# Copies for the weight sums moved to the weight queue, their additions queued stage by stage behind POOL's steps

## The chip, the cores and the metric

The kernel runs on one core of a Trainium2 chip. A core has a matrix engine (TensorE, PE in the profile; its weight loads are PEld), a vector engine (DVE), a scalar engine (ACT), a general engine (POOL) and SyncE (SP), which here only issues transfers. Each engine takes its instructions in a fixed order. Transfers (DMAs) are issued from an engine's queue and carried out by 16 shared DMA engines. The metric is the device time of one execution in microseconds (us), as the median of several runs.

## The reference

One decoder layer on 512 tokens of width 2048 in float32, with two groups of heads side by side:

```python
mod = silu(c) @ w_ada + b_ada                       # shift, scale, gate
u = rms_norm(x) * norm_w * (1 + scale) + shift
z, xbc, dt, q, k, v, g = split(u @ w_in)            # w_in is 2048 x 11296
xbc = silu(causal_conv(xbc)); xs, B, C = split(xbc)
y = ssd_scan(xs, softplus(dt + dt_bias), -exp(a_log), B, C) + xs * d_skip
y_ssd = group_rms_norm(y * silu(z)) * ssd_norm_w    # 4 groups of 8 heads
o = retention(rotary(q), rotary(k), v)              # 8 heads, chunks of 128
y_ret = head_norm(o) * ret_norm_w * silu(g)
h = x + gate * (concat(y_ssd, y_ret) @ w_out)       # w_out is 4096 x 2048
out = rms_norm(h) * final_norm_w
```

## The kernel before

**Matrix products.** Every large product is made of three matmuls (`mm3`, L107 to L109): each operand is split into a high part and a low remainder, hi·hi, hi·lo and lo·hi. `load_w` (L93) brings 512 KB of weights with one SP transfer into `raw` (3 buffers), ACT casts it to `hi` (L98), and DVE subtracts to get `lo` (L99; 4 buffers each).

**Stages.** First the modulation vectors, and with them, as far as the activations are ready, the first products (B, C, xs and z of group 0, lines L223 to L277). Then the heads' work. `unit` (L111) is one projection of 512 columns, eight loads of weights and 192 matmuls of 512 columns. For SSD group g: the units xs and z, `ssd_a(g)` (the scan over four chunks: a decay tile loaded by POOL from `acs_d` at L401 and masked at L402, subtracted and multiplied on DVE at L404 and L407, then the matmuls py L419, po L423, pst L432 with `xw` from POOL at L430), and `ssd_b(g)` (gate, square root on POOL at L75 and L76, and `put_mix`, L337, which transposes the result, forms block differences on POOL and stores them to DRAM from POOL's queue). For each pair p of retention heads: the unit qk, `ret_a(p)` (rotary on DVE with an addition on POOL, L468, transposes pk L482, scores), the unit v beside which the gate's weights are loaded, `ret_b(p)` (chunks; a normalisation `mv` on POOL at L75 and L76, state products pkv L537), the unit g, and `ret_c(p)` (gate and `put_mix`). Before the first scan, cumulative decays are computed, transposed and copied to `acsT` (L644), and POOL stores them to `acs_d` in DRAM (L646).

**The output projection** takes `w_out` in 2 x 2 blocks and needs seven block products in place of eight. For that it wants sums of weight blocks, for each of 16 column-by-row pieces j: T1 = B11 + B12, T3 = B12 + B22, T2 = T1 + B22, T4 = T2 + B21. These are made by transfers alone, DRAM to DRAM, 512 KB each: a copy, then transfers that add to their destination, which go through POOL's queue. `block_sums(n)` (L362) issues six stages, one per tick, for pieces n to n − 5: SP copies T1 and T3 (L369); POOL adds to both (L366); POOL copies T1 to T2 (L371); adds (L366); copies T2 to T4 (L373); adds (L366). `unit` calls it at every sixth of its loading steps, over all units counted through.

**Order.** The program order is a priority: a planner lays out each engine's instructions ahead of time from its own estimates of when each is ready, and the engines then run these lists in order. `tc.issue_after(ins)` holds the instructions traced in its block, as far as they are on the engine of `ins`, behind `ins` in that engine's list, without waiting for it to finish. At L122 `ins` is the SP load just issued, so only the SP copies are held by it, and POOL's steps of the sums are placed by the planner.

Of the kernel before, what the change touches and what calls it, by code (L numbers as in the profile page):

```python
# [41 lines left out]
def hybrid_block(ctx, tc, x, c_row, vecs, heads, w_mod, w_gate, b_gate, w_in, w_dt, w_out, fnw,  # L42
                 rope, dmask, xi, zeta, gdec, out):
    nc = tc.nc
    act, dve, pool, pe, sp = nc.scalar, nc.vector, nc.gpsimd, nc.tensor, nc.sync
# [45 lines left out]
    last_load = [None]  # L91
# [19 lines left out]
    def unit(name, w_stationary, tag="mm", side=None):  # L111
        width = 512
        nb = width // P if w_stationary else NC
        banks = [bank(tag, f"acc{b}") for b in range(nb)]
        held = []
        for kc in range(NK // 2):
            held.append((kc, *load_w(w_in[name][kc], width)))
            if side is not None:
                side(kc)
            n = next(steps)  # L120
            if n % 6 == 0:
                with tc.issue_after(last_load[0].ins):  # L122
                    block_sums(n // 6)
            if kc == NK // 2 - 2:
                continue
            for b in range(nb):
                sl = slice(b * P, (b + 1) * P)
                for k, hi, lo in [(2 * c + kt, h[:, kt, :], l[:, kt, :])
                                  for c, h, l in held for kt in range(2)]:
                    if w_stationary:  # L130
                        mm3(banks[b], (hi[:, sl], lo[:, sl]), (uh[k], ul[k]),
                            k == 0, k == NK - 1)
                    else:
                        mm3(banks[b][:, :width], (uh[k][:, sl], ul[k][:, sl]), (hi, lo),
                            k == 0, k == NK - 1)
            held = []
        return banks
# [183 lines left out]
    QJ = 8  # L321
# [4 lines left out]
    B11, B12, B22, B21 = (lambda j, i=i: w_out[4 * j + i] for i in range(4))  # L326
# [32 lines left out]
        pool.dma_start(mixd["SA"][j][:, 1, :], a12)  # L359
        pool.dma_start(mixd["A22"][j // 2][:, j % 2, :], a22)  # L360

    def block_sums(n):  # L362


        def add(dst, src):
            pool.dma_start(dst, src, accum_op=ALU.add, max_dma_last_dim=4096)  # L366

        stages = (
            lambda j: (sp.dma_start(T1(j), B11(j)), sp.dma_start(T3(j), B12(j))),  # L369
            lambda j: (add(T1(j), B12(j)), add(T3(j), B22(j))),  # L370
            lambda j: pool.dma_start(T2(j), T1(j)),  # L371
            lambda j: add(T2(j), B22(j)),
            lambda j: pool.dma_start(T4(j), T2(j)),  # L373
            lambda j: add(T4(j), B21(j)))
        for i, stage in enumerate(stages):
            if 0 <= n - i < 2 * QJ:
                stage(n - i)

    steps = iter(range(10000))


    def ssd_a(g):
        bt, ct, xs = bct[("B", g)], bct[("C", g)], xst[g]
        hs = slice(g * HPG, (g + 1) * HPG)
        pb = bank("aux", "pb")
        for c in range(NC - 1):
            pe.transpose(pb[:, c * P:(c + 1) * P], bt[:, c * P:(c + 1) * P], ident)
        bn = t2k("bn", 2, "bn")
        act.copy(bn[:, 0:3 * P], pb[:, 0:3 * P])
        pcb = bank("aux", "pcb")  # L390
        for c in range(NC):
            sl = slice(c * P, (c + 1) * P)
            pe.matmul(pcb[:, sl], lhsT=bt[:, sl], rhs=ct[:, sl], start=True, stop=True)
        cbt = t2k("cbt", 2, "cbt")
        act.copy(cbt, pcb)
        prev = None
        ys = []
        for c in range(NC):
            sl = slice(c * P, (c + 1) * P)
            dec = t2k("dec", 2, "dec", (P, HPG, P))  # L400
            pool.dma_start(dec, acs_d[c, hs, :].partition_broadcast(P))  # L401
            pool.affine_select(dec, dec, [[0, HPG], [1, P]], ALU.is_ge, -1e30, base=0,  # L402
                               channel_multiplier=-1)
            dve.tensor_tensor(dec, dec, acs[:, c, hs].unsqueeze(2).to_broadcast([P, HPG, P]),  # L404
                              ALU.subtract)
            act.activation(dec, dec, AF.Exp)
            dve.tensor_tensor(dec, dec, cbt[:, sl].unsqueeze(1).to_broadcast([P, HPG, P]), ALU.mult)  # L407
            px = bank("aux", "px")
            for i in range(4):
                pe.transpose(px[:, i * P:(i + 1) * P], xs[i][:, sl], ident)  # L410
            xd = t2k("xd", 2, "xd")
            dve.tensor_tensor(v8(xd), v8(px), bcast_h(dtt[:, c, hs]), ALU.mult)
            xc = t2k("xc", 2, "xc")
            act.copy(xc, px)
            pool.tensor_tensor(v8(xc), v8(xc), bcast_h(dsk[:, hs]), ALU.mult)
            py = bank("aux", "py")
            for h in range(HPG):
                hd = slice(h * 64, (h + 1) * 64)
                pe.matmul(py[:, hd], lhsT=dec[:, h, :], rhs=xd[:, hd], start=True, stop=True)  # L419
            y = t2k("y", 4, "y")  # L420
            if c:
                po = bank("aux", "po")
                pe.matmul(po, lhsT=ct[:, sl], rhs=prev, start=True, stop=True)  # L423
                dve.tensor_tensor(v8(y), v8(po), bcast_h(ea[:, c, hs]), ALU.mult)
                pool.tensor_tensor(xc, xc, y, ALU.add)
            dve.tensor_tensor(y, py, xc, ALU.add)
            ys.append(y)
            if c < NC - 1:
                xw = t2k("xw", 2, "xw")
                pool.tensor_tensor(v8(xw), v8(xd), bcast_h(dte[:, c, hs]), ALU.mult)  # L430
                pst = bank("aux", "pst")
                pe.matmul(pst, lhsT=bn[:, sl], rhs=xw, start=True, stop=True)  # L432
                new = t2k("prev", 2, "new")
                if c == 0:
                    act.copy(new, pst)
                else:
                    pool.tensor_tensor(v8(new), v8(prev), bcast_h(cdec[:, c, hs]), ALU.mult)
                    dve.tensor_tensor(new, pst, new, ALU.add)
                prev = new
        return ys  # L440

    def silu2(pb, name, zs=None):
        th = t2k("th", 2, "th")
        act.activation(th, pb, AF.Tanh, scale=0.5)
        if zs is None:
            zs = t2k("zs", 4, name)
        dve.scalar_tensor_tensor(zs, th, 1.0, pb, ALU.add, ALU.mult)  # L447
        return zs

    def ssd_b(g, ys, zss):  # L450
        sq = small.tile([P, NC], F32, name="sq")
        for c in range(NC):
            y = ys[c]
            dve.tensor_tensor(y, y, zss[c], ALU.mult)
            act.activation(zss[c], y, AF.Square, accum_out=sq[:, c:c + 1])
            rsqrt_into(sq[:, c:c + 1], sq[:, c:c + 1], 1.0 / 2048.0, EPS)
            dve.tensor_scalar(y, y, sq[:, c:c + 1], None, ALU.mult)
        for i in range(4):
            put_mix(4 * g + i, [y[:, i * P:(i + 1) * P] for y in ys], hv(V_SNW, 4 * g + i))
# [106 lines left out]
    def gate_part(n, q):  # L566
        raw = wp.tile([P, 2, 512], F32, tag="raw", bufs=3, name="graw")
        sp.dma_start(raw.rearrange("p k f -> p (k f)"), w_gate[8 * n + q])
        if n % 2 == 0 and q == 0:
            gates["t"] = t2k("dec", 2, "gacc", (P, HPG, P)).rearrange("p (a h) t -> p a (h t)", a=2)  # L570
        if q == 0:
            gates[n] = gates["t"][:, n % 2, :]
        gacc = gates[n]
        for kk in range(2):
            k = 2 * q + kk
            if k == 0:
                dve.tensor_scalar(gacc, raw[:, kk, :], cs[:, k:k + 1], None, ALU.mult)
            else:
                dve.scalar_tensor_tensor(gacc, raw[:, kk, :], cs[:, k:k + 1], gacc,  # L579
                                         ALU.mult, ALU.add)  # L580
# [11 lines left out]
    zs0 = []  # L592
# [59 lines left out]
    for j in range(2):  # L652
        bct[("B", j)] = conv_silu(None, 16 + j, "bc", 5, f"B{j}", aw[j])
        bct[("C", j)] = conv_silu(None, 20 + j, "bc", 5, f"C{j}", aw[2 + j])
    ssd_b(0, ssd_a(0), zs0)
    for g in range(1, GROUPS):
        if g == 2:
            take_bc(unit("BC2", True), 2)
        take_xs(unit(f"xs{g}", True), g)
        ys = ssd_a(g)  # L660
        zb = unit(f"z{g}", False)
        ssd_b(g, ys, [silu2(zb[c], f"zs{c}") for c in range(NC)])
    for p in range(RH // 2):
        qk = unit(f"qk{p}", True)
        a = ret_a(p, qk)
        vb = unit(f"v{p}", False, side=lambda kc: gate_part(p, kc))
        gate_done(p)
        ys = ret_b(p, a, vb)
        gb = unit(f"g{p}", False)
        ret_c(p, ys, gb)  # L670


    gate = []
# [228 lines left out]
```

## Time and profile before

| | |
|---|---|
| runs | 1552.52, 1552.04, 1546.27 us; median 1552.04 |
| profiled execution | 1547.64 us, its span 1545.9 us |
| busy | TensorE 1450.1 us (94%), DVE 890.8 (58%), ACT 539.5 (35%), POOL 395.0 (26%) |
| mean granted TensorE clock | 0.979 of full speed |
| transfers | 324.09 MB; SP's queue 245.52 MB, POOL's 75.37 MB |
| DMA engines' busy share | SP's queue 46.3%, POOL's 20.1% |

A line of the tables of waits names the waiting engine and instruction, what released it, the total in us, how often, and the longest. A line of the timeline gives start, duration, engine, source line, operation, output<-inputs, and in brackets the idle time ahead of it with what ended it. A stretch's line gives its bounds and length, the busy time of PE, PEld, DVE, ACT and POOL, the granted clock, the DMA engines' busy share and GB/s. Of a transfer's issue the profile gives the size and the median time to landing.

### The profile page before, as it was taken

The page shows a single profiled execution, that of the slowest core. Times are in us where ns is not written, and L with a number is a line of the kernel's source. Part 1 is how long each engine was busy: PE and PEld are TensorE (multiplying, and loading weights), DVE is VectorE, ACT ScalarE, POOL GpSimd, SP SyncE. Part 2 cuts the span into 40 slices and gives each one's busy share as a digit, 9 for nine tenths or more (in the row PEclk, how much of TensorE's full clock was granted, in tenths as well). Part 3 has the DMA queues.
Part 4 walks back from the last instruction along what each step waited for, and adds up shares of the span by engine and source line. Part 5 has one row for each costly group of instructions (what it writes and reads, how often), then busy time and mean ns, then how long its engine had stood idle before and what let it go on. Part 6 is the DMA issues. An engine that isn't in the chain of part 4 may idle for free.

```text
span 1545.9 us, 17183 instructions
## 1 busy us (share of the span) xinstructions
PE 1450.1 (94%) x6481; PEld 1177.1 (76%) x6481; DVE 890.8 (58%) x1064; ACT 539.5 (35%) x732; POOL 395.0 (26%) x472
## 2 busy tenths in 40 slices
PE   6989996898999999988998999999999999999997
PEld 4767884686877877766887888788878878888885
DVE  6899764855655455363326433743354456557585
ACT  6433442432433332211121222122222345546454
POOL 4540114565425515432143003200310020000001
PEclk9999997999999999999999999999999999999998
DMA  9887786386787775688687525523553588778755
GB/s 363 321 303 282 226 239 176 116 245 183 216 232 202 228 214 147 211 245 249 182 228 224 159 82 170 172 80 96 171 170 119 166 307 286 248 242 264 248 177 196
DMA packets 86263, 324.09 MB, mean 210 GB/s; under 512 B 11298, under 2 KB 11474, under 8 KB 81058
## 3 DMA queue, kind: packets, MB, share of 16 engines
q1 hardware_dynamic: 66834, 245.52, 46.3%
q0 software_dynamic: 18192, 75.37, 20.1%
q10 hardware_dynamic: 1152, 2.10, 0.4%
q8 instruction: 51, 0.84, 0.2%
q14 instruction: 34, 0.27, 0.0%
HBM read 304.00 MB, written 86.05 MB: 252 GB/s over the span
## 4 chain that ended last, share of the span: by engine, by line
PE 52%; DMA 22%; DVE 13%; issue 6%; POOL 5%; ACT 2%; SPq 0%; DVEq 0%; POOLq 0%; ACTq 0%
PE acc L108 9%; PE acc L107 9%; PE acc L109 9%; DMA T<-w_out_d 9%; DMA graw<-w_gate_d 5%; DVE ada L193 4%; DMA T<-T 4%; PE U L108 4%; PE U L109 4%; PE U L107 3%; PE W L107 3%; PE W L108 3%; PE W L109 3%; DVE lo L99 2%; DVE ul L210 1%
## 5 line engine op out<-in xcount | busy, mean ns | idle before, releaser
L98 ACT CAST hi<-raw 128x1024 fp32r<-128x1024 f32 (+1 forms) x184 | 186.1, 1016 | 448.6 <-PE acc L109 198.7
L99 DVE TENSOR_TENSOR lo<-raw,hi 128x1024 fp32r<-128x1024 f32 (+1 forms) x166 | 211.3, 1277 | 223.8 <-ACT hi L98 223.2
L107 PE MATMUL acc<-hi,uh 128*128 128x512 f32 x704 | 277.5, 396 | 11.0 <-DVE rt L467 10.7
L108 PE MATMUL acc<-lo,uh 128*128 128x512 f32 x704 | 280.2, 398 | 0.0
L109 PE MATMUL acc<-hi,ul 128*128 128x512 f32 x704 | 279.0, 396 | 0.0
L109 PE MATMUL acc<-uh,lo 128*128 128x512 f32 x512 | 201.0, 393 | 0.0
L107 PE MATMUL acc<-uh,hi 128*128 128x512 f32 x512 | 200.7, 394 | 0.3 <-DVE zs L447 0.3
L108 PE MATMUL acc<-ul,hi 128*128 128x512 f32 x512 | 200.7, 392 | 0.0
L735 DVE TENSOR_TENSOR lo<-raw,hi 128x1024 fp32r<-128x1024 f32 x112 | 137.6, 1234 | 81.2 <-ACT hi L734 81.2
L107 PEld LDWEIGHTS acc<-hi,uh 128*128 128x128 f32 x704 | 133.3, 189 | 41.0 <-DVE rt L467 13.0
L734 ACT CAST hi<-raw 128x1024 fp32r<-128x1024 f32 x112 | 117.6, 1054 | 126.7 <-PE W L109 53.8
L109 PEld LDWEIGHTS acc<-hi,ul 128*128 128x128 f32 x704 | 133.6, 190 | 27.9 <-issue 0.2
L108 PEld LDWEIGHTS acc<-lo,uh 128*128 128x128 f32 x704 | 133.6, 190 | 27.9 <-issue 0.5
L107 PEld LDWEIGHTS acc<-uh,hi 128*128 128x128 f32 x512 | 96.6, 189 | 20.9 <-DVE zs L447 1.5
L109 PEld LDWEIGHTS acc<-uh,lo 128*128 128x128 f32 x512 | 96.7, 189 | 19.6
L108 PEld LDWEIGHTS acc<-ul,hi 128*128 128x128 f32 x512 | 96.5, 188 | 19.5
L366 POOL DMA_DIRECT2D T<-w_out_d x64 | 55.3, 886 | 212.4 <-DMA T<-T 107.3
L108 PE MATMUL U<-lo,mh 128*128 128x512 f32 x256 | 99.8, 390 | 0.8 <-DVE lo L735 0.8
L109 PE MATMUL U<-hi,ml 128*128 128x512 f32 x256 | 99.6, 390 | 0.0
L107 PE MATMUL U<-hi,mh 128*128 128x512 f32 x256 | 95.2, 390 | 0.0
L579 DVE SCALAR_TENSOR_TENSOR gacc<-graw,cs,gacc 128x512 f32<-128x512 f32 x60 | 49.4, 823 | 79.2 <-DMA graw<-w_gate_d 78.0
L193 DVE SCALAR_TENSOR_TENSOR ada<-ada,csb 128x2048 f32<-128x2048 f32 x32 | 91.0, 2845 | 0.2 <-DMA ada<-w_mod_d 0.2
(245 smaller groups left out, 2199.8 us busy)
## 6 DMA issues: line engine op xcount, KB each, us to landing
ada<-w_mod_d SPq DMA_DIRECT2D x32, 1024.0 KB, 6.1
T<-w_out_d POOLq DMA_DIRECT2D x64, 512.0 KB, 6.8
raw<-T SPq DMA_DIRECT2D x64, 512.0 KB, 4.3
raw<-w_out_d SPq DMA_DIRECT2D x48, 512.0 KB, 4.4
raw<-w_in_z SPq DMA_DIRECT2D x32, 512.0 KB, 5.1
T<-w_out_d SPq DMA_DIRECT2D x32, 512.0 KB, 6.4
T<-T POOLq DMA_DIRECT2D x32, 512.0 KB, 5.0
raw<-w_in_qk SPq DMA_DIRECT2D x32, 512.0 KB, 3.7
```

Of the source, the lines that this page charges most:

```text
L98: act.copy(hi, raw)
L99: eng.tensor_tensor(lo, raw, hi.bitcast(F32), ALU.subtract)
L107: pe.matmul(dst, lhsT=ah, rhs=bh, start=first, stop=False, skip_group_check=more)
L108: pe.matmul(dst, lhsT=ah, rhs=bl, start=False, stop=False, skip_group_check=more)
L109: pe.matmul(dst, lhsT=al, rhs=bh, start=False, stop=last, skip_group_check=more)
L193: dve.scalar_tensor_tensor(ada, ada, 0.5, csb, ALU.mult, ALU.mult, accum_out=dst)
L210: dve.tensor_tensor(l_k, xT[k], h_k.bitcast(F32), ALU.subtract)
L366: pool.dma_start(dst, src, accum_op=ALU.add, max_dma_last_dim=4096)
L579: dve.scalar_tensor_tensor(gacc, raw[:, kk, :], cs[:, k:k + 1], gacc, ALU.mult, ALU.add)
L734: act.copy(dst[0], src)
L735: dve.tensor_tensor(dst[1], src, dst[0].bitcast(F32), ALU.subtract)
```

## The change

The call of `block_sums` leaves `unit`. It is made instead after each part of the heads' work: `ssd_a`, `ssd_b`, `ret_a`, `ret_b`, `ret_c`, 20 calls (ticks) in all. The six stages become four. At its first tick a piece j has all four T filled by SP copies straight from the weights: T1 from B11, T3 from B12, T2 from B22, T4 from B21. At the second POOL adds B12 to T1 and B22 to T3, at the third T1 to T2, at the fourth T2 to T4. A helper `behind(eng)` finds the instruction last traced on an engine: the copies are held behind SP's last one, the additions behind POOL's last one. Tick 14 issues pieces 14 and 15 together.

```diff
@@ unit
-            n = next(steps)
-            if n % 6 == 0:
-                with tc.issue_after(last_load[0].ins):
-                    block_sums(n // 6)
@@ block_sums
-    def block_sums(n):
+    ticks = iter(range(1000))
+    def behind(eng):
+        ins = next(i for i in reversed(nc.cur_bb.bb.instructions) if i.engine == eng.engine)
+        return tc.issue_after(ins)
+    def block_sums():
         def add(dst, src):
             pool.dma_start(dst, src, accum_op=ALU.add, max_dma_last_dim=4096)
-        stages = (
-            lambda j: (sp.dma_start(T1(j), B11(j)), sp.dma_start(T3(j), B12(j))),
-            lambda j: (add(T1(j), B12(j)), add(T3(j), B22(j))),
-            lambda j: pool.dma_start(T2(j), T1(j)),
-            lambda j: add(T2(j), B22(j)),
-            lambda j: pool.dma_start(T4(j), T2(j)),
-            lambda j: add(T4(j), B21(j)))
-        for i, stage in enumerate(stages):
-            if 0 <= n - i < 2 * QJ:
-                stage(n - i)
-    steps = iter(range(10000))
+        n = next(ticks)
+        for i in range(4):
+            for j in {14: (14, 15)}.get(n - i, (n - i,)):
+                if not 0 <= j < 2 * QJ or n - i > 14:
+                    continue
+                if i == 0:
+                    with behind(sp):
+                        for dst, src in ((T1, B11), (T3, B12), (T2, B22), (T4, B21)):
+                            sp.dma_start(dst(j), src(j))
+                else:
+                    with behind(pool):
+                        if i == 1:
+                            add(T1(j), B12(j))
+                            add(T3(j), B22(j))
+                        elif i == 2:
+                            add(T2(j), T1(j))
+                        else:
+                            add(T4(j), T2(j))
@@ the heads' work
-    ssd_b(0, ssd_a(0), zs0)
+    ys = ssd_a(0)
+    block_sums()
+    ssd_b(0, ys, zs0)
+    block_sums()
     for g in range(1, GROUPS):
...
         ys = ssd_a(g)
+        block_sums()
...
         ssd_b(g, ys, [silu2(zb[c], f"zs{c}") for c in range(NC)])
+        block_sums()
     for p in range(RH // 2):
         qk = unit(f"qk{p}", True)
         a = ret_a(p, qk)
+        block_sums()
...
         ys = ret_b(p, a, vb)
+        block_sums()
         gb = unit(f"g{p}", False)
         ret_c(p, ys, gb)
+        block_sums()
```

## The prediction

> **What bounds the kernel now.** I read the page first: its busy shares, and the chain that ended last by line.
>
> ```profile
> span 1545.9 us, 17183 instructions
> PE 1450.1 (94%) x6481; PEld 1177.1 (76%) x6481; DVE 890.8 (58%) x1064; ACT 539.5 (35%) x732; POOL 395.0 (26%) x472
> ...
> PE acc L108 9%; PE acc L107 9%; PE acc L109 9%; DMA T<-w_out_d 9%; DMA graw<-w_gate_d 5%; DVE ada L193 4%; DMA T<-T 4%; PE U L108 4%; PE U L109 4%; PE U L107 3%; PE W L107 3%; PE W L108 3%; PE W L109 3%; DVE lo L99 2%; DVE ul L210 1%
> ```
>
> TensorE is the bound: 94% busy, and no change to the sums removes a matmul. What can be won is idle TensorE time, 95.8 us in all, and time at a lower clock. The chain, though, runs 13% of the span through transfers into T (9% from the weights, 4% from T to T), which only the output projection reads. So I asked next who waits for T, when T is written and read (the instructions of that tile, with the start of the first and the last), and where TensorE's idle time lies, in stretches cut at the stages.
>
> ```profile
> POOL T L366 <- DMA T<-T: 107.3, 26, 7.0
> POOL T L366 <- DMA T<-w_out_d: 104.5, 20, 19.3
> ...
> POOL T L373 <- DMA T<-w_out_d: 69.8, 16, 6.3
> POOL T L371 <- DMA T<-w_out_d: 55.4, 15, 9.5
> ```
>
> ```profile
> L366 POOL DMA_DIRECT2D T<-w_out_d x64: 797/864/1422, 177.7 to 847.1; - x64
> L739 SPq DMA_DIRECT2D raw<-T x64: 319/320/430, 1214.8 to 1509.0; - x64
> ```
>
> ```profile
> 160.00:236.00 76.00, 76.00 (x349) 62.85 (x349) 51.96 (x80) 31.57 (x47) 12.50 (x20) 1.00 0.79 230
> 236.00:300.00 64.00, 43.37 (x200) 33.52 (x199) 45.11 (x48) 21.71 (x31) 34.05 (x38) 0.84 0.51 132
> 300.00:420.00 120.00, 112.54 (x526) 90.46 (x525) 70.94 (x70) 42.83 (x63) 68.36 (x81) 0.97 0.74 216
> 420.00:555.00 135.00, 131.96 (x622) 107.39 (x622) 73.74 (x86) 51.16 (x72) 52.48 (x67) 0.99 0.79 224
> 555.00:650.00 95.00, 89.98 (x420) 71.57 (x419) 40.44 (x46) 27.39 (x38) 43.13 (x54) 0.98 0.66 184
> 650.00:860.00 210.00, 192.94 (x850) 157.69 (x849) 99.67 (x124) 41.41 (x47) 55.42 (x72) 0.97 0.77 223
> 860.00:1240.00 380.00, 375.22 (x1695) 309.95 (x1694) 175.04 (x246) 98.11 (x119) 59.24 (x79) 1.00 0.43 138
> ```
>
> POOL stands 337.0 us in its queue before T steps (107.3 + 104.5 + 69.8 + 55.4). Columns after the stretch: its length, busy PE, PEld, DVE, ACT, POOL, granted clock, DMA share, GB/s. TensorE idles 20.6, 7.5, 3.0, 5.0 and 17.1 us in the five stretches from 236 to 860, and its clock is below 1 in each. From 860 on, after POOL's last T step at 847, the retention heads do the same kind of work with 4.8 us idle in 380 us at a clock of 1.00. That is a control inside this trace: without T steps in POOL's queue the heads hardly stop TensorE. Last, what TensorE waited for from 160 to 1250:
>
> ```profile
> PE py L419 <- DVE dec L407: 15.2, 1, 15.2
> PE pst L432 <- POOL xw L430: 10.7, 6, 4.4
> PE acc L107 <- DVE rt L467: 10.7, 7, 2.6
> PE pT L342 <- DVE y L457: 7.2, 5, 3.8
> PE pkv L537 <- DVE yr L529: 6.3, 1, 6.3
> PE pk L482 <- POOL r L468: 4.8, 4, 2.0
> ```
>
> The largest is one wait, and the timeline shows its cause.
>
> ```profile
> 219.00 0.27 ACT L644 COPY acsT<-pat 128x128 f32<-128x128 f32 x1
> ...
> 235.27 0.80 POOL L366 DMA_DIRECT2D T<-w_out_d  x1 [6.47 <-DMA T<-T]
> 235.80 0.86 POOL L646 DMA_DIRECT2D acs_d<-acsT  x1
> 241.55 1.08 POOL L401 DMA_DIRECT2D dec<-acs_d  x2 [4.89 <-DMA acs_d<-acsT]
> ...
> 251.74 3.67 PE L419 MATMUL py<-xd,dec 128*128 128x64 f32 x16 [15.18 <-DVE dec L407]
> ...
> 283.53 2.00 PE L419 MATMUL py<-xd,dec 128*128 128x64 f32 x16 [0.89 <-DVE xd L412]
> ```
>
> acsT is ready at 219.3, but its store (L646) stands in POOL's queue behind T steps, each waiting some 6 us for the one before, until 235.8: 16.5 us late. The decay tiles and the first py follow from it.
>
> **The change part by part.** *The six-step chain becomes four, and 32 T-to-T copies leave POOL.* T2 and T4 start as copies of B22 and B21 on SP; POOL then adds T1 and T2. Still 64 copies and 64 additions of 512 KB: the transfers' bytes do not change.
>
> ```profile
> L366 POOL DMA_DIRECT2D T<-w_out_d x64 | 55.3, 886 | 212.4 <-DMA T<-T 107.3 <-DMA T<-w_out_d 104.5 <-issue 0.5
> ...
> L373 POOL DMA_DIRECT2D T<-T x16 | 8.6, 540 | 69.8 <-DMA T<-w_out_d 69.8
> L371 POOL DMA_DIRECT2D T<-T x16 | 8.5, 529 | 55.4 <-DMA T<-w_out_d 55.4
> ...
> T<-w_out_d POOLq DMA_DIRECT2D x64, 512.0 KB, 6.8
> ...
> T<-w_out_d SPq DMA_DIRECT2D x32, 512.0 KB, 6.4
> ```
>
> POOL loses 17.1 us of issue (8.6 + 8.5), worth nothing by itself on an engine 26% busy, and the 125.2 us of waits before these copies.
>
> *The additions go behind POOL's last step of each part, one stage a tick.* From tick 1 on a projection unit lies between two ticks, 192 matmuls, some 42 us at the 349 in 76.0 us of 160:236; an addition lands in a median 6.8 us, so every input has long landed. I cost POOL's waits for T at nothing; the cover is that spacing, and if two ticks fell together each stage would wait up to 6.8 us again. At tick 0 POOL gets no addition, so L646 issues when acsT is there, at about 219.3. Then the store, loads, mask and decay (251.7 − 235.8 = 15.9 us in the trace) give py at 235.2, just before TensorE runs out of other work at 236.6 (251.74 − 15.18). So **15.2 us** of idle go, and the slow restart: 16 py take 3.67 us there and 2.00 later, with the steps behind them about **2.5**.
>
> *The other SSD stalls.* pst waits for xw on POOL 10.7 us; two of the six had no T wait in front of them, so 10.7 − 0.45 − 1.35 = **8.9** go.
>
> ```profile
> 276.30 1.12 PE L432 MATMUL pst<-xw,bn 128*128 128x512 f32 x2 [0.45 <-POOL xw L430]
> ...
> 595.24 1.13 PE L432 MATMUL pst<-xw,bn 128*128 128x512 f32 x2 [1.35 <-POOL xw L430]
> ```
>
> pT waits 7.2 for a normalisation whose square root is on POOL; I credit half, **3.6**. Clock, (1 − clock) × stretch: 3.6 in 300:420, 1.4 in 420:555, 1.9 in 555:650, and, as an estimate of the same size, 1.6 in 236:300 after pT's longest stall of 3.8: **8.5**.
>
> *The first four heads.* 650:860 against its control: idle 17.1 − 4.8 = **12.3** and clock 0.03 × 210 = **6.3**. pkv's 6.3 and the excess in rt and pk are inside this.
>
> Sum of what can go: 15.2 + 2.5 + 8.9 + 3.6 + 8.5 + 12.3 + 6.3 = 57.3 us. The Trainium skill (TensorE: Matmul & The Clock Gate, Part 1) has the clock halve after an idle window of about 3.4 us; by that only the four longest stalls would cost clock, and the sum would be some 5 us smaller (an estimate); but 420:555, with no such gap among its waits, also shows 0.99.
>
> *What it adds: bursts on SP.* Ticks 0 and 1 both stand behind the last load of the first stage, so eight copies, 4.2 MB, go ahead of the xs1 weights; tick 14 also sends eight, the others four.
>
> ```profile
> 168.03 0.33 SPq L95 DMA_DIRECT2D raw<-w_in_xs0b  x1
> 168.63 0.33 SPq L95 DMA_DIRECT2D raw<-w_in_xs  x1
> 169.01 2.84 SPq L369 DMA_DIRECT2D T<-w_out_d  x2
> ...
> 190.19 0.50 PE L107 MATMUL acc<-uh,hi 128*128 128x512 f32 x1
> ...
> 193.03 1.13 SPq L369 DMA_DIRECT2D T<-w_out_d  x2
> ```
>
> The first xs1 load was issued at 168.6 and first used at 190.2: 21.6 us of cover, less about 2.3 for the cast and the subtraction. At the 230 GB/s of 160:236 the eight take 18.2 us. 168.6 + 18.2 + the load's own 2.3 at that rate, + 2.3, makes 191.4: 1 us late, and ACT, held in its cast, may pass it on to acsT. Bounds: 0 (the POOL transfers that shared those 230 GB/s are gone) and 5; I take 2. Later bursts of four take 9.1 us with a like cover: 0.
>
> *What waits behind the additions.* Four take about 3.5 us (4 × 0.886; tick 15 has six, behind ret_b). After ssd_a their successors are ssd_b's square roots, three times (groups 1 to 3), and TensorE waits for those in pT: 0 to 10.5, taken at 5, since the z unit's matmuls cover part. After ret_a, ret_b, ssd_b and ret_c a whole projection unit covers them: 0. The T steps now reach into 860 to about 1130, where the DMA share was 0.43. The first read of T is at 1215, so nothing in the output projection becomes late.
>
> *What passes to the next releaser.* A stalled head often has DVE or ACT a little behind POOL; of the 42.1 us other than the first stall I take off a fifth, 8.
>
> 57.3 − 2 − 5 − 8 = 42 us. The profiled execution took 1547.6 us (span 1545.9 and 1.7 around it): 1547.6 − 42 = 1505.6. The median of the runs shown is 4.4 us above that execution, so I add 2: **1508 us**.
>
> **The rivals.** *Only the first stall goes* (1540): POOL's waits elsewhere hid DVE and ACT chains, and the additions cost their whole 10.5. For it: four of the six rows of TensorE's waits name DVE, not POOL. Against it: the control. 1547.6 − 17.7 + 10.5 is 1540.4.
>
> *The transfers bind and nothing moves* (1548): same bytes, share 0.74 to 0.79 in three of the stretches; waits for T become waits for weights. Against it: TensorE's list of waits names no load. The skill (DMA: Bandwidth & Descriptors, Issuing engines are not separate DMA queues) speaks for it: handing transfers to another issuer saves only issue time.
>
> *The bursts starve TensorE* (1645, slower): the place is the first weights behind a burst. If each copy is served alone in its 6.4 us, four take 25.6 and eight 51.2. Against 19.3 us of cover (21.6 − 2.3) that is 6.3 us in each of the 12 bursts of four and 31.9 in each of the two of eight: 139; 1505.6 + 139 = 1645. It decides from 4.9 us a copy (12 × 0.3 + 2 × 19.9 = 43, the whole gain). Against it: 230 GB/s makes 2.3 us a copy, and pairs issued together, two in 1.13 us, have that 6.4 as their median.
>
> **How the numbers follow.** Forecast 0.62, first stall only 0.18, nothing moves 0.09, starved 0.11. Within 0.5% of 1552 is about what a measurement can tell from no change; so faster 0.80, same 0.09, slower 0.11. The likeliest case's own range is 1490 (all 57.3) to 1530. For 8 in 10 it reaches over the first-stall case to 1546, and down to 1486 for a planner that places the freed work better.
>
> **What would show it.** Right: no T-to-T transfer on POOL, POOL's waits for T below 40 us, L646 within 2 us of acsT, no PE wait above 5 us from 236 to 860, clock 1.00 at 650:860. Wrong step by step: a PE wait for hi or lo near 190 (burst); pT waits above 7.2 us (additions ahead of ssd_b); py still over 10 us late (the order of the planner, not T). The whole is wrong if POOL's waits vanish and TensorE's idle time does not.

## The result and the profile after

| | before | after |
|---|---|---|
| median, us (runs) | 1551.0 (4, 1546.27 to 1552.52) | 1492.65 (4, 1489.38 to 1496.37) |
| profiled execution, us | 1547.64 | 1496.37 |
| its span, us | 1545.9 | 1494.7 |
| mean granted TensorE clock | 0.979 | 0.987 |

The ratio of after to before is 0.963, 95% interval 0.960 to 0.966: 58.4 us between the medians, 51.3 between the two profiled executions. The forecast of 1508 us had the direction and the mechanism, and its range (1486 to 1546) holds the result; the gain was larger than the 42 us worked out.

The page of after, its busy shares and the shares of the chain that ended last by line:

```profile
span 1494.7 us, 17196 instructions
PE 1438.2 (96%) x6481; PEld 1174.4 (79%) x6481; DVE 895.1 (60%) x1064; ACT 540.2 (36%) x732; POOL 377.2 (25%) x440
...
PE acc L108 13%; PE acc L107 13%; PE acc L109 13%; DMA graw<-w_gate_d 5%; DVE ada L189 4%; PE U L108 3%; PE U L109 3%; PE U L107 3%; PE W L107 2%; PE W L108 2%; PE W L109 2%; DVE gacc L588 1%; DVE lo L99 1%; PE py L428 1%; DVE ul L206 1%
```

Transfers into T, which held 13% of the chain, are no longer among the lines listed. TensorE's idle time fell from 95.8 to 56.5 us (1494.7 − 1438.2). Where it went shows in the stretches, before and then after. The bounds are cut at the same stages; columns as in the prediction.

```profile
236.00:860.00 624.00, 570.79 (x2613) 460.62 (x2612) 329.91 (x371) 184.50 (x250) 253.44 (x312) 0.96 0.72 206
860.00:1240.00 380.00, 375.22 (x1695) 309.95 (x1694) 175.04 (x246) 98.11 (x119) 59.24 (x79) 1.00 0.43 138
1240.00:1545.90 305.90, 291.97 (x1279) 240.67 (x1277) 195.83 (x216) 155.22 (x204) 12.33 (x20) 0.98 0.74 245
```

```profile
160.00:236.00 76.00, 76.00 (x349) 63.02 (x348) 55.92 (x85) 34.09 (x50) 10.49 (x14) 1.00 0.59 208
236.00:300.00 64.00, 59.19 (x295) 47.62 (x295) 48.13 (x53) 27.30 (x41) 36.97 (x41) 0.97 0.42 146
300.00:404.00 104.00, 103.83 (x494) 85.08 (x493) 65.71 (x67) 40.76 (x57) 51.07 (x59) 1.00 0.67 194
404.00:530.00 126.00, 126.00 (x607) 103.66 (x606) 76.53 (x85) 49.50 (x70) 45.40 (x56) 1.00 0.63 193
530.00:620.00 90.00, 88.64 (x427) 72.40 (x426) 47.15 (x53) 26.66 (x36) 41.99 (x52) 1.00 0.67 192
620.00:810.00 190.00, 183.48 (x821) 149.60 (x819) 89.11 (x113) 38.65 (x45) 45.01 (x56) 0.99 0.74 217
...
236.00:810.00 574.00, 561.13 (x2637) 458.37 (x2636) 326.62 (x368) 182.87 (x248) 220.43 (x261) 0.99 0.66 196
810.00:1188.00 378.00, 372.62 (x1671) 308.71 (x1672) 178.91 (x246) 97.85 (x119) 77.16 (x103) 0.99 0.63 187
1188.00:1494.70 306.70, 292.39 (x1278) 240.45 (x1276) 195.65 (x216) 155.25 (x204) 11.59 (x19) 0.98 0.75 245
```

From 236 to the end of the heads both kernels run the same 4308 matmuls (2613 + 1695, 2637 + 1671), in 1004 us before and 952 after: 52.0 us. The output projection took 0.8 us longer, and everything before 236 is unchanged. Of the 52.0, idle time gave 39.7 (53.2 + 4.8 before, 12.9 + 5.4 after), and the remaining 12.3 is shorter busy time of the same matmuls; how much of it is clock is worked out below.

The list of TensorE's waits after, from 150 to 1195, and then the one row of a T step in the list of POOL's waits:

```profile
PE acc L107 <- DVE rt L476: 6.4, 6, 2.3
PE pT L338 <- DVE y L433: 4.6, 1, 4.6
PE pk L491 <- POOL r L477: 2.8, 1, 2.8
PE acc L107 <- ACT hi L98: 2.4, 2, 1.2
...
PE acc L108 <- DVE lo L99: 1.5, 2, 0.8
```

```profile
POOL T L369 <- DMA mixAS<-m: 1.6, 1, 1.6
```

The rest of the list are waits of 1.9 us or less in total; py's 15.2, pst's 10.7 and pkv's 6.3 us have no successor in it. The rows for `hi` and `lo`, 3.9 us of waits for weights, are new: they come at 656 and at 809, in the first two v units, behind bursts of four copies. POOL's 337.0 us of waits for T are gone: the 1.6 us ahead of a T step are not for a transfer that makes T. (The list also puts POOL's 48.4 us ahead of `cosb`, until 165.7, down to a transfer into T. The same wait was 47.4 us long before, put down to DVE there, so it is not a new one.) The timeline of after at the first scan, to be held against the one in the prediction:

```profile
221.65 0.27 ACT L653 COPY acsT<-pat 128x128 f32<-128x128 f32 x1 [2.23 <-PE pat L651]
222.21 0.55 POOL L655 DMA_DIRECT2D acs_d<-acsT  x1 [52.65 <-ACT acsT L653]
...
238.78 1.90 PE L428 MATMUL py<-xd,dec 128*128 128x64 f32 x16
```

POOL now waits for acsT (52.7 us, harmless) instead of acsT waiting for POOL. The store goes 0.3 us after acsT, and py runs without an idle gap and at full speed: 1.90 us for the sixteen, 3.67 before.

### The profile page after: what moved, and what is told of

It is laid out like the page before. It is cut to its first block, busy times and chain, and to the rows that moved or that the text cites. A ratio compares the mean times of both kernels' runs of the same rounds, so it can differ in the third digit from the quotient of the medians.

```text
span 1494.7 us, 17196 instructions
## 1 busy us (share of the span) xinstructions
PE 1438.2 (96%) x6481; PEld 1174.4 (79%) x6481; DVE 895.1 (60%) x1064; ACT 540.2 (36%) x732; POOL 377.2 (25%) x440
## 4 chain that ended last, share of the span: by engine, by line
PE 64%; DVE 13%; DMA 10%; issue 8%; POOL 3%; ACT 1%; SPq 1%; DVEq 0%; POOLq 0%; ACTq 0%
PE acc L108 13%; PE acc L107 13%; PE acc L109 13%; DMA graw<-w_gate_d 5%; DVE ada L189 4%; PE U L108 3%; PE U L109 3%; PE U L107 3%; PE W L107 2%; PE W L108 2%; PE W L109 2%; DVE gacc L588 1%; DVE lo L99 1%; PE py L428 1%; DVE ul L206 1%
## 5 line engine op out<-in xcount | busy, mean ns | idle before, releaser
L109 PEld LDWEIGHTS acc<-uh,lo 128*128 128x128 f32 x512 | 96.2, 188 | 19.3
L588 DVE SCALAR_TENSOR_TENSOR gacc<-graw,cs,gacc 128x512 f32<-128x512 f32 x60 | 54.2, 904 | 73.2 <-DMA graw<-w_gate_d 72.1
L108 PE MATMUL W<-lo,mh 128*128 128x512 f32 x192 | 75.6, 394 | 0.1
```

Of the source, the lines that this page charges most:

```text
L108: pe.matmul(dst, lhsT=ah, rhs=bl, start=False, stop=False, skip_group_check=more)
L109: pe.matmul(dst, lhsT=al, rhs=bh, start=False, stop=last, skip_group_check=more)
```

## The experiments

Two edits came together: the chain of six stages became four, and the steps moved from the counter in `unit` to ticks between the parts, with POOL's additions held behind POOL's last step. The first four runs take these apart and take the sums away; the next four look at where the waits stand and at the bursts of copies. All ratios are to the kernel before (median 1549.31 beside the first four, 1550.84 beside the others), with their 95% intervals.

**Six stages at the new place.**

```diff
-        for i in range(4):
+        for i in range(6):
...
-                        for dst, src in ((T1, B11), (T3, B12), (T2, B22), (T4, B21)):
+                        for dst, src in ((T1, B11), (T3, B12)):
...
                         elif i == 2:
-                            add(T2(j), T1(j))
-                        else:
-                            add(T4(j), T2(j))
+                            pool.dma_start(T2(j), T1(j))
+                        elif i == 3:
+                            add(T2(j), B22(j))
+                        elif i == 4:
+                            pool.dma_start(T4(j), T2(j))
+                        else:
+                            add(T4(j), B21(j))
```

> The new places with the old chain: ticks after each part and additions (with both T-to-T copies) held behind POOL's last step, but six stages, so 32 copies stay on POOL. Theory A (what counts is that nothing in POOL's queue waits for a transfer just issued; every stage's input is one part old): POOL's waits for T stay below 40 us, TensorE's idle time as in the changed kernel; 1493 to 1500 us, the 17 us of issue for the copies lying off the path. Rival B (the shorter chain and the copies taken off POOL are the gain): well above, 1520 to 1540 us.

Measured 1492.47 us, ratio 0.963 (0.959 to 0.967): the changed kernel's time, and rival B is out. With the long chain, and its 32 copies still on POOL, the one wait ahead of a T step is this, and no transfer ends it:

```profile
POOL T L369 <- issue: 0.9, 2, 0.5
```

So the shorter chain, and the 32 copies that went from POOL to SP, are worth nothing once the steps stand at the new place, behind POOL's last step. That is also what the Trainium skill says of such a move (DMA: Bandwidth & Descriptors, Issuing engines are not separate DMA queues: it saves only issue time), and here the trace agrees. What it was used for in the prediction's second rival doesn't follow, though: the gain never lay in the issuer.

**Four stages at the old place.**

```diff
-            lambda j: (sp.dma_start(T1(j), B11(j)), sp.dma_start(T3(j), B12(j))),
+            lambda j: [sp.dma_start(d(j), s(j)) for d, s in ((T1, B11), (T3, B12), (T2, B22), (T4, B21))],
             lambda j: (add(T1(j), B12(j)), add(T3(j), B22(j))),
-            lambda j: pool.dma_start(T2(j), T1(j)),
-            lambda j: add(T2(j), B22(j)),
-            lambda j: pool.dma_start(T4(j), T2(j)),
-            lambda j: add(T4(j), B21(j)))
+            lambda j: add(T2(j), T1(j)),
+            lambda j: add(T4(j), T2(j)))
```

> The four-stage chain alone, called from the units' loading steps as before, additions placed by the planner. Theory A: two of six waits per piece are gone, POOL still stands some 200 us for T and still holds up the store of acsT; 1515 to 1535 us. Rival B: 1490 to 1500 us.

Measured 1518.69 us, ratio 0.976 (0.970 to 0.983): 31 us less, about half of the change. The size is uncertain, 27 to 46 us by the interval, and its four runs lie between 1504.55 and 1528.23. POOL's waits, the first scan, and TensorE's stretch over it:

```profile
POOL T L366 <- DMA T<-w_out_d: 206.8, 39, 21.0
...
POOL T L366 <- DMA T<-T: 78.5, 14, 8.2
```

```profile
219.17 0.60 POOL L644 DMA_DIRECT2D acs_d<-acsT  x1 [0.71 <-ACT acsT L642]
...
236.01 1.90 PE L417 MATMUL py<-xd,dec 128*128 128x64 f32 x16
```

```profile
236.00:300.00 64.00, 58.41 (x286) 46.88 (x285) 43.67 (x51) 26.43 (x39) 35.75 (x37) 0.95 0.56 159
```

POOL still waits 285.3 us for T, more than the 200 expected. But it does not hold up the store of acsT, as was expected: the shorter chain was over just as acsT came, and the first sixteen py run at 236.0, without a gap and at full speed, where they came at 251.7 before. TensorE idles 5.6 us from 236 to 300 in place of 20.6. With the steps where the planner puts them, then, a shorter chain counts; some 15 of its 31 us of gain come from this one meeting, which is a matter of timing.

**The ticks without the hold on POOL.** The additions are no longer held behind POOL's last step; the planner places them. SP's copies stay as they were.

```diff
                 else:
-                    with behind(pool):
+                    with nullcontext():
```

> The changed kernel with the additions not held behind POOL's last step (ticks, four stages and SP's holds kept). Theory A: the planner may put an addition as soon as its own estimate of the transfer is over, earlier than the chip lands it; POOL's waits for T come back in part, 50 to 200 us, and 1500 to 1530 us. Rival C (the tick after a part is enough, the hold adds nothing): 1490 to 1497 us.

Measured 1502.47 us, ratio 0.969 (0.965 to 0.974), 10 us above the changed kernel.

```profile
POOL T L369 <- DMA T<-w_out_d: 160.7, 32, 24.4
POOL T L369 <- DMA T<-T: 56.6, 10, 7.6
```

The planner brings the additions forward, and POOL waits 217.3 us, a little more than the 50 to 200 expected. Little of that reaches TensorE. The time is inside theory A's range, and the four runs (1498.41 to 1503.9) lie above all four of the changed kernel, so rival C is out.

**No sums at all.** The transfers into T are gone, and the output projection reads B11, B22, B12 and B21 where it read T1 to T4: the same loads and matmuls on other numbers.

```diff
-            n = next(steps)
-            if n % 6 == 0:
-                with tc.issue_after(last_load[0].ins):
-                    block_sums(n // 6)
...
-    for sweep, (f, wu, ww) in enumerate((("AS", B11, T1), ("SR", T2, B22), ("SA", T3, B21))):
+    for sweep, (f, wu, ww) in enumerate((("AS", B11, B11), ("SR", B22, B22), ("SA", B12, B21))):
...
-        held.append((j, m, weight(T4(j))))
+        held.append((j, m, weight(B21(j))))
```

> The kernel before with no block sums at all: the 128 transfers into T are left out, and the projection reads the weight blocks B11, B22, B12 and B21 where it read T1 to T4, so the output is not the reference's. It gives the price of the sums. Theory A: the changed kernel hides nearly all of it, so this is 1482 to 1492 us, at most 10 us under the changed kernel. Rival D (the transfers' bytes bind, and the changed kernel still pays for 64 copies and 64 additions): below 1475 us.

Measured 1490.67 us, ratio 0.961 (0.958 to 0.965). The sums cost the kernel before some 59 us and the changed one about 2, which is inside the spread of its runs. The rival in which the bytes bind is out: 128 transfers of 512 KB are hidden, once no urgent work stands in line behind them. There is hardly anything left to win in the sums.

**The old steps, four ticks later.** This moves the first steps from 177.7 to 326.6, past the first scan, and changes nothing else.

```diff
-                    block_sums(n // 6)
+                    block_sums(n // 6 - 4)
```

> The kernel before with its sums begun four ticks (24 loading steps) later, so that none stands ahead of the store of acsT; six stages, old places, planner's positions. It isolates the first stall. Theory A (two terms, the first stall with its restart and the waits inside the later parts): the first wait of 15 us goes, the others move to later groups and heads; 1525 to 1537 us. Rival E (the first stall is nearly the whole): 1495 to 1510 us. Rival F (a stall avoided there returns elsewhere): 1545 us or more.

Measured 1538.04 us, ratio 0.993 (0.990 to 0.997), 1 us above theory A's range; rivals E and F are out. Rows of the waits of POOL and TensorE, and the two stretches:

```profile
POOL acs_d L646 <- ACT acsT L644: 50.5, 1, 50.5
...
PE pkv L537 <- DVE yr L529: 15.5, 2, 10.9
```

```profile
236.00:860.00 624.00, 589.83 (x2725) 478.37 (x2723) 327.83 (x378) 189.13 (x256) 240.58 (x296) 0.98 0.71 205
860.00:1190.00 330.00, 311.45 (x1383) 256.84 (x1384) 146.79 (x211) 73.80 (x87) 66.58 (x92) 0.97 0.55 163
```

The store of acsT is in time, so the first stall is gone, which the prediction priced at 17.7 us. The kernel gains only 10 (1 − 0.9934 of 1551) to 13 (the medians). The last of POOL's T steps now comes at 985, in heads that were free of them before, and the largest wait of TensorE is now pkv's, 15.5 us in place of 6.3. There, from 860 to 1190, TensorE idles 18.6 us, against 4.8 in the whole 860:1240 of before. The same heads with T steps in POOL's list stall, without them they don't; this is the prediction's control, now made by an edit.

**Sixteen copies at once.** SP's copies of four pieces go out together at ticks 0, 4, 8 and 12; the additions stay.

```diff
-            for j in {14: (14, 15)}.get(n - i, (n - i,)):
-                if not 0 <= j < 2 * QJ or n - i > 14:
+            js = {14: (14, 15)}.get(n - i, (n - i,) if n - i < 14 else ())
+            if i == 0:
+                js = range(n, n + 4) if n % 4 == 0 else ()
+            for j in js:
+                if not 0 <= j < 2 * QJ:
                     continue
```

> The changed kernel with the copies of four pieces, 16 transfers or 8.4 MB, sent together at ticks 0, 4, 8 and 12; the additions as in the changed kernel. It prices the cover ahead of the weights. By the prediction's figures 16 copies at 230 GB/s take 36.5 us against 19.3 us of cover: some 17 us lost at each of four bursts, 1545 to 1565 us. If copies are served at their packets' pace when nothing else runs (4 KB in 0.159 us on each of 16 engines, 1.3 us a copy), 16 take 20 us and the loss is small: 1493 to 1500 us. If each copy were served alone in its landing time of 6 to 8 us, 80 us or more would be lost at each burst: above 1700 us.

Measured 1519.0 us, ratio 0.979 (0.976 to 0.983): 26 us slower than the changed kernel, and in none of the three ranges. The lines of SP's queue at the first burst, TensorE's timeline behind the first and behind a later one, the list of its waits, and the stretch while the first burst drains:

```profile
158.36 3.13 SPq L382 DMA_DIRECT2D T<-w_out_d  x5
...
169.09 12.56 SPq L382 DMA_DIRECT2D T<-w_out_d  x11
182.60 26.18 SPq L95 DMA_DIRECT2D raw<-w_in_xs  x8
```

```profile
195.86 0.79 PE L107 MATMUL acc<-uh,hi 128*128 128x512 f32 x1 [4.92 <-ACT hi L98]
...
822.99 2.08 PE L107 MATMUL acc<-hi,uh 128*128 128x512 f32 x4 [8.67 <-ACT hi L98]
```

```profile
PE acc L107 <- ACT hi L98: 24.8, 5, 8.7
```

```profile
160.00:180.00 20.00, 20.00 (x89) 16.41 (x88) 15.23 (x21) 6.88 (x9) 3.81 (x7) 1.00 0.97 341
```

The starvation that the third rival feared exists: weights behind a burst come late and TensorE waits for them, 24.8 us in all. But the size of a burst alone doesn't decide it. Behind the first burst TensorE waits 4.9 us, behind the second, at 379, not at all, behind the third and fourth, around the v units, 8.2 and 11.7; and in the changed kernel 3.9 us follow bursts of four. The price of a copy lies below both that the prediction worked with (and near the 1.3 of the second range): 341 GB/s while the queue is full makes 1.5 us for 512 KB (2.3 at the 230 GB/s of before, 6.4 if served alone). At that price sixteen need some 25 us, more than the prediction's 19.3 us of cover, and eight need 12, less than it. (Five of the first sixteen went ahead of a load again, so this is an estimate of the size, no working of each stall. Why the second burst is free stays open.)

**Six stages at the ticks, without the hold.** The first experiment with the third one's edit.

```diff
                 else:
-                    with behind(pool):
+                    with nullcontext():
```

> Ticks after each part, with six stages and without the hold on POOL: the ticks alone. Theory A': the gain from where the ticks stand and the gain from the hold add up, and the chain's length matters only where the planner sets the places; 1505 to 1525 us, with POOL's waits for T at 300 us or more. Rival C: 1490 to 1500 us, ticks alone are enough.

Measured 1530.05 us, ratio 0.987 (0.982 to 0.991): rival C is out, but theory A' missed as well, by 5 us above its range. POOL's waits for T (the lines of the two copies and of the additions):

```profile
POOL T L369 <- DMA T<-T: 103.2, 27, 6.6
POOL T L386 <- DMA T<-w_out_d: 65.7, 16, 9.8
POOL T L390 <- DMA T<-w_out_d: 62.6, 14, 8.1
POOL T L369 <- DMA T<-w_out_d: 55.3, 16, 15.5
```

These are 286.8 us, where 300 or more were expected. The hold is worth 38 us with six stages, where it was worth 10 with four; the ticks alone give 21. So what the hold is worth depends on the length of the chain: at the ticks two stages more cost 28 us without it and nothing with it.

**All additions of a piece at one tick.** T1 + B12, T3 + B22, T2 + T1 and T4 + T2 stand at the same tick, held behind POOL's last step, so each depends on one issued shortly before.

```diff
-        for i in range(4):
+        for i in range(2):
...
                     with behind(pool):
-                        if i == 1:
-                            add(T1(j), B12(j))
-                            add(T3(j), B22(j))
-                        elif i == 2:
-                            add(T2(j), T1(j))
-                        else:
-                            add(T4(j), T2(j))
+                        add(T1(j), B12(j))
+                        add(T3(j), B22(j))
+                        add(T2(j), T1(j))
+                        add(T4(j), T2(j))
```

> The changed kernel with all four additions of a piece issued at one tick, each waiting for the one before, still held behind POOL's last step of the part. POOL gets its waits back, 14 to 25 us at each of 15 ticks, 200 to 350 us in all, but at the ends of parts. Theory G (the place of a wait decides, not its length: what follows on POOL is not wanted until a projection later): 1493 to 1508 us, the losses only where ssd_b's square roots stand behind it. Theory A as predicted (waits in POOL's queue cost, and the spacing of the stages is the cover): 1515 to 1550 us.

Measured 1495.72 us, ratio 0.964 (0.960 to 0.968).

```profile
POOL T L369 <- DMA T<-T: 96.5, 14, 11.2
POOL T L369 <- DMA T<-w_out_d: 54.8, 12, 8.8
```

POOL waits 151.3 us for T again, fewer than the 200 to 350 expected; the hold only says "behind", and in the timeline the planner still puts other work between the additions. The time is 3 us above the changed kernel, within the spread of either's runs, so theory G holds and theory A's range is missed.

All kernels with the spaced copies in one table (us; the hold is that on POOL's steps):

| stages | steps placed | POOL's waits for T | median | above no sums |
|---|---|---|---|---|
| six | counter in `unit`, no hold (before) | 337.0 | 1551.0 | 60 |
| six | the same, four ticks later | 380.2 | 1538.0 | 47 |
| six | ticks, no hold | 286.8 | 1530.1 | 39 |
| four | counter in `unit`, no hold | 285.3 | 1518.7 | 28 |
| four | ticks, no hold | 217.3 | 1502.5 | 12 |
| four, all additions at one tick | ticks, hold | 151.3 | 1495.7 | 5 |
| four | ticks, hold (after) | 0 | 1492.7 | 2 |
| six | ticks, hold | 0 | 1492.5 | 2 |
| none | | 0 | 1490.7 | 0 |

(380.2 is 157.0 + 97.5 + 75.8 + 49.9 in the list of POOL's waits of that run; waits that were not ended by a transfer that makes T are left out in all rows, 1.6 us in after and 0.9 in the run below it among them.) More waiting mostly goes with more time, but not in proportion. 151.3 us cost 5, the next 66 cost 7, and the 50 from 286.8 to 337.0, six stages both, cost 21. And it isn't the length alone: 380.2 cost 13 us less than 337.0, and two kernels with the same 286 differ by some 11, at the edge of what their runs can tell. What a wait costs depends on what stands behind it in POOL's list: that is shown for the first stall, and fits the rest.

## Why the prediction was right, and where it was not

**The cause.** Right. TensorE idled because POOL's list held other engines' inputs behind its waits for T. The run without the hold, the later start and the run without sums each move the time the way this asks, and the rivals with the bytes or the first stall alone are out: 40.7 of the 58.4 us came beyond the 17.7 at which the first stall was priced. Of the signs, the store 0.3 us behind acsT, no wait above 4.6 us from 236 to 860 and the end of POOL's waits for T came. "No T-to-T transfer on POOL" could not: the 32 copies are gone, but the additions of T1 to T2 and of T2 to T4 are T-to-T transfers too.

**First stall, 15.2 and 2.5.** Right in the trace of after: store 0.3 us behind acsT, py 16.6 us behind the store (15.9 assumed), no wait, 1.90 us for the sixteen. By itself, in the later start, the step is worth less only because the steps went elsewhere.

**pst and pT, 8.9 and 3.6.** With the first stall they make 27.7 us of idle time from 236 to 650. Measured: 36.1 before (20.6 + 7.5 + 3.0 + 5.0), 6.3 after (4.8 + 0.2 + 0.0 + 1.4), so 29.8. No wait for xw is left, and of pT's one of 4.6 and one of 0.2.

**First four heads, 12.3 of idle.** 17.1 before, 6.5 after: 10.6, though the cut of this stretch is a few matmuls off. Two errors lie in this term. It took off the control's whole 4.8 us, which belong to 380 us; for 210 us they are 2.6, so 14.4 could go. And of the 6.5 that are left 3.9 are the new waits for weights; without them 2.6, as in the control. All idle terms together: 40.0 predicted, 39.7 measured, but it is luck that they agree so closely.

**Clock, 8.5 + 6.3 + 2.5 = 17.3.** Too large: 12.3 was there, at most. From 236 to 860 the trace of before has eight stretches of 3.4 to 17.1 us in which the granted clock is 0.50, with 31.4 us of TensorE's work in them, so 15.7 lost; after has four of 3.4 us up to 1188 (at 272, 658, 812 and 1078), with 12.9 us of work, 6.5 lost. The term was some 2 us above what there was to lose, and left out that the changed kernel has slow stretches of its own. 9.2 us went; the other 3.1 have no row. The clock of the first heads came to 0.99, not to the 1.00 named as the sign. The rule of the Trainium skill that the prediction weighed (TensorE: Matmul & The Clock Gate, Part 1) put the sum at 5 us less, 52.3 (an estimate); 52.0 came. The trace agrees with the halving, and with 3.4 us as the shortest stretch, but not with the gap that is to bring it about, so the total comes near by luck. Here two pst of before behind a gap of 2.27 us, and the stretch that they start:

```profile
462.78 2.07 PE L432 MATMUL pst<-xw,bn 128*128 128x512 f32 x2 [2.27 <-POOL xw L430]
```

```profile
462.30:465.70 3.40, 2.92 (x7) 1.78 (x8) 0.69 (x1) 0.59 (x1) 2.07 (x4) 0.50 0.98 186
```

They take 2.07 us, against 1.13 behind the 1.35 us at 595 that the prediction shows.

**The three deductions, 2, 5 and 8.** This is the step that failed: 57.3 − 2 − 5 − 8 made 42, and 52.0 came, 57.3 less 5.0 of clock and 0.3 of idle time. Each has its row.

- *The burst of eight, 2.* As written, both ticks stand behind the last load of the first stage. In SP's queue after, five of the copies had gone ahead of that load:

```profile
158.08 3.16 SPq L379 DMA_DIRECT2D T<-w_out_d  x5
168.41 0.34 SPq L95 DMA_DIRECT2D raw<-w_in_xs0b  x1
168.79 3.67 SPq L379 DMA_DIRECT2D T<-w_out_d  x3
```

```profile
ACT hi L98 <- DMA raw<-w_in_xs: 3.1, 2, 2.7
```

  ACT was indeed held in its cast, 2.7 us at the longest (the second fence, from the list of waits of 160:222), and acsT came 2.6 us later than before. That the one made the other is not shown: with sixteen copies at this place the copy to acsT starts at 217.4, against 221.7 here and 219.0 before. In any case TensorE had work through it, 76.00 of 76.00 us busy from 160 to 236, and the cost was 0. The price of 2.3 us a copy was too high as well. Behind the later bursts of four, put at 0, come the 3.9 us of waits for weights, in two v units, beside which the gate's weights are loaded too. Neither the kernel before nor the run without sums has these waits. The run with all additions at one tick has the same bursts and 0.3 us, so what makes them stays open.
- *Additions ahead of the square roots, 5.* 0. In the timeline of after, in group 1, the square root waits for its own input when the additions have long been issued:

```profile
341.95 1.72 POOL L369 DMA_DIRECT2D T<-w_out_d  x2
343.10 1.41 POOL L369 DMA_DIRECT2D T<-T  x1
...
347.02 0.34 POOL L75 TENSOR_SCALAR sq<-sq 128x1 f32<-128x1 f32 x1 [1.40 <-ACT zs L464]
```

  The one pT wait that is left, 4.6 us, lies at 272, before the first addition (299.9); after it all waits in pT come to 0.2.
- *What passes to the next releaser, 8.* 0, on the whole: the idle time went as summed. TensorE's largest wait for DVE, rt, fell from 10.7 us to 6.4, near the 5.8 of the run without sums. The fifth had been taken without a row for it.

**POOL's waits for T at nothing, with spacing as the cover.** The waits went, 1.6 us left, but the cover named was not needed: with all additions of a piece at one tick POOL waits 151.3 us and the kernel keeps its time to 3 us. What counts is that the steps come behind the urgent work, and the spacing is a second safety.

**The medians.** The 51.3 us between the profiled executions became 58.4 between the medians: the execution of before lies 3.4 us below its median, that of after 3.7 above. The 2 us added for the kernel before went the right way for it and the wrong way here.

**The rivals.** Only the first stall: 1540, out by 47 us. Nothing moves: out by the result, and the run without sums shows that the bytes are hidden. Starved: its mechanism was shown with sixteen copies, at some 1.5 us a copy, far from the 4.9 from which it would have decided with four and eight. Whether the changed kernel's 3.9 us are the same thing stays open.

## What to carry to other kernels

A transfer whose input is another transfer made its engine's whole list wait here, so ask of each such step what stands behind it, and put it behind that; how long it then waits mattered little (151.3 us, about 3 us of time). Price such a change from a stretch of the same trace in which the same work runs without the suspect steps, scaled to the same length, and deduct only what has a row of its own. Two ways of easing one wait don't add: at the new ticks the shorter chain alone is worth 28 us and the hold alone 38, and both together 37.

## What the runs showed that was not expected

- The additions landed later in the changed kernel than before, and it cost nothing. The rows of the profile's list of transfers after (KB each, median us from issue to landing), where the additions from the weights took 6.8 before:

```profile
T<-w_out_d POOLq DMA_DIRECT2D x32, 512.0 KB, 8.8
T<-T POOLq DMA_DIRECT2D x32, 512.0 KB, 13.6
```

  The last is issued at 1071.6 and T is first read at 1162.5, so there were some 90 us for it to land in.
- With sixteen copies and the loads queued, the DMA engines moved 341 GB/s at a busy share of 0.97; the 230 GB/s at 0.79 that the prediction took as the rate of a copy was the mean of a stretch in which they were not always busy and which held additions as well.
- 151 us of waits on one engine cost 3 us of time, while 16.5 us by which one store was late made TensorE idle for 15.2.
